# The last projection of the long sequence without Strassen, the order of the jobs around it, and the small steps of four norms on other engines

## The chip, the cores and the metric

The kernel runs on one core of a Trainium2 chip. The metric is the device time of one execution, in microseconds (us); lower is better. The engines are TensorE (PE in the profile; PEld is its weight load), VectorE (DVE), ScalarE (ACT), GpSimd (POOL) and SyncE (SP), which issues the transfers.

## The reference

Two requests pass through the same two layers with shared weights: a prompt of 512 positions (called Q in the kernel) and a sample of 1024 positions (S). The width is 1024. Cut to what matters:

```python
def even_layer(x, ...):                       # layer one
    p = rms_norm(x, g_norm) @ w_in            # value, GLU gate, Fourier input, two gates
    a = a_val * sigmoid(a_glu)
    a = depthwise_conv_centred(a, conv_w)     # 31 taps
    a = silu(layer_norm(a)) * silu(a_z)
    f = real(fft2 over positions and group channels) @ w_four * silu(f_z)
    return x + concatenate([a, f]) @ w_out    # w1o in the kernel

def odd_layer(x, ...):                        # layer two
    u, bg, cg, z = split(rms_norm(x, g_norm) @ w_in, 4)        # w2
    v = depthwise_conv_centred(cg * u, conv_w)                 # 3 taps
    return x + (bg * v * silu(z)) @ w_out                      # w2o

y = rms_norm(odd_layer(even_layer(x)))        # for the prompt and for the sample
```

All of it is in float32.

## The kernel before

**Tiles and precision.** Activations are kept transposed: channels on the 128 partitions, 512 positions (a chunk) along a tile. Q has one chunk and S two. A width of 1024 is 8 such tiles. Each operand of a matmul is split in two parts of a faster format, a high one (a cast on ScalarE, L116 for activations, L144 for weights) and a low one (a subtraction, on VectorE at L110 for activations and on GpSimd at L145 for weights). A product is the sum of high·high, high·low and low·high. So one output tile (`project`, L174 to L190, names `one`, `o`, `val`, `glu`) takes 3 × 8 = 24 matmuls of 128x512. With `kind=1` these are ordered by the input tile k, so that the operands of the last k are needed last.

**Strassen.** For S some projections are done as `Pair` (L656 to L740): two output tiles for both chunks with the Winograd form of Strassen's algorithm, 7 products of 12 matmuls, 84 instead of 96. It needs sums of operands and of weights (VectorE, names `as`, `bs`, `ys`) and sums of results (X, Y, Z at L710, then `xr`). The operands of product p lie in buffer rings by the table `HOME`.

**Order.** The program is written as a list of jobs (`One` for a plain tile, `Pair` for Strassen). `run` (L745) walks through it, loads and splits weights some steps ahead, and advances late generators (vector work of other stages) at given step numbers. A scheduler then places the instructions, and each engine runs its own in order. The jobs are, in the order of the list:

- layer one of Q and S (inputs, 31-tap convolution `conv31`, Fourier part), with Q's output projection
- four groups (j = 0 to 3) of Q's layer-two input, `l2_in`, of four tiles each
- `l1_out_two`: S's output projection of layer one, four pairs
- the other four groups of `l2_in`
- `l2_two`: S's layer-two input, 16 pairs, with the 3-tap convolution and gates
- `l2_out_first`: three tiles of Q's last projection
- `l2_out_two`: S's last projection, four pairs
- `l2_out_last`: Q's other five tiles, each in two halves of 256 columns, so that the first half's final norm runs beside the second half's matmuls. S's final norm (`fin`, 16 output tiles) runs beside them too.

**Norms.** A norm's squares are summed over tiles on ScalarE and VectorE (`SqSum`). `rstd_begin` (L201) sums them over channels by matmuls with a column of ones (`cs`, L209), takes the reciprocal root by a bit trick and three Newton steps on VectorE (12 instructions on at most 8 columns, L214 to L221, ahead of others by priority), and scales a 128x128 identity by it (`d`, L226, one instruction per 128 positions). `rstd_end` (L237) spreads the root over all partitions by a matmul (`r`), and `norm_apply` (L261) scales the tiles. `norm_mid` (L598) is Q's norm between the layers; `layer_norm` (L547) is the one after the 31-tap convolution.

## Time and profile before

| | us |
|---|---|
| median of three runs | 1206.56 |
| lowest and highest | 1206.23, 1209.15 |
| the profiled execution | 1205.27 |
| its span in the trace | 1203.5 |
| PE busy | 1139.1 (95%) |
| DVE busy | 910.3 (76%) |
| POOL busy | 538.7 (45%) |
| ACT busy | 475.3 (39%) |

A row of the timeline gives the start, the duration, the engine, the line, the operation, output<-inputs with their shape, how many such instructions follow each other, and in square brackets the idle time before it with what ended it. In the table of windows each stretch of the span (us) has its length, then for each engine its busy time with the number of instructions, the granted TensorE clock (1 is full), the busy share of the DMA engines and the GB/s that they moved. A row of waits names who waited for whom: us in total, how often, and the longest. In a row that groups instructions stand their count, busy time, mean ns of one, and the idle time before them with what ended it.

The stages in the trace, by window: 150 to 175 us is S's second input norm; 440 to 541 the first four groups of Q's layer-two input; 541 to 627 `l1_out_two`; 627 to 715 the other four groups; 715 to 1034 `l2_two`; 1034 to 1061 the three tiles `l2_out_first`; 1061 to 1145 `l2_out_two`; 1145 to 1184 `l2_out_last`; then the tail.

### The profile page before, as it was taken

Reading aid. Unit: us, or ns where it says so; the run is one execution under the profiler, and the core shown is the slowest. Engines: PE = TensorE matmul, PEld = TensorE weight load, DVE = VectorE, ACT = ScalarE, POOL = GpSimd, SP = SyncE. Lnnn points to the kernel's source line nnn. Section 1 sums busy time; section 2 is a strip of 40 time slices with the busy share of each in tenths; the row PEclk is TensorE's granted clock in tenths of the full one; section 3 lists DMA queues with packets and bytes.
Section 4 is the critical chain, followed back from the end, with each engine's and each line's share of the span. In section 5 each row is a group of like instructions: output and inputs, shape, how many; then the busy total and the mean of one; then the engine's idle time right before and its main releaser. Section 6 shows DMA issues by size and latency. Waiting matters only on the chain. (4 is left out here: it accounts for less than half of the span.)

```text
span 1203.5 us, 15117 instructions
## 1 busy us (share of the span) xinstructions
PE 1139.1 (95%) x5160; PEld 932.6 (77%) x5160; DVE 910.3 (76%) x1306; ACT 475.3 (39%) x827; POOL 538.7 (45%) x396
## 2 busy tenths in 40 slices
PE   7999989999999989997999998999999999979994
PEld 6778868888988868875878876888888888758793
DVE  5899988999899977697564887655546556896756
ACT  6543532223344244443342444333333333643531
POOL 3442532122265535465434544544444544344452
PEclk9999989999999999998999998999999999999997
DMA  9323211111236575355463563221222444766648
GB/s 324 124 95 116 88 53 47 42 53 53 89 106 202 166 243 182 99 185 173 155 219 128 170 211 127 79 88 53 79 71 79 139 133 165 232 208 215 198 155 288
DMA packets 94541, 169.33 MB, mean 141 GB/s; under 512 B 10496, under 2 KB 14080, under 8 KB 94464
## 3 DMA queue, kind: packets, MB, share of 16 engines
q1 hardware_dynamic: 94176, 168.08, 42.9%
q8 instruction: 40, 0.66, 0.2%
q14 instruction: 37, 0.30, 0.1%
q10 hardware_dynamic: 288, 0.30, 0.1%
HBM read 132.94 MB, written 35.39 MB: 140 GB/s over the span
## 5 line engine op out<-in xcount | busy, mean ns | idle before, releaser
L145 POOL TENSOR_TENSOR wo<-wf,wo 128x512 fp32r<-128x512 f32 x254 | 358.1, 1425 | 470.6 <-ACT wo L144 324.7
L144 ACT CAST wo<-wf 128x512 fp32r<-128x512 f32 x256 | 150.1, 618 | 220.5 <-PE X L710 56.2
L145 POOL TENSOR_TENSOR wo<-as,wo 128x512 fp32r<-128x512 f32 x96 | 134.0, 1396 | 136.3 <-ACT wo L144 130.0
L537 DVE SCALAR_TENSOR_TENSOR cv<-a,par_sb,cv 128x1024 f32<-128x1024 f32 x120 | 154.3, 1286 | 2.4 <-ACT cv L535 0.5
L144 ACT CAST wo<-as 128x512 fp32r<-128x512 f32 x96 | 59.3, 618 | 149.0 <-PE X L710 86.9
L710 PE MATMUL X<-ysh,wo 128*128 128x512 f32 x256 | 87.1, 405 | 14.3 <-DVE xr L110 8.0
L537 DVE SCALAR_TENSOR_TENSOR cv<-ap,par_sb,cv 128x512 f32<-128x512 f32 x120 | 90.3, 753 | 2.1
L710 PE MATMUL X<-bsh,wo 128*128 128x512 f32 x256 | 85.0, 393 | 0.0
L110 DVE TENSOR_TENSOR acc<-acc,sq 128x512 f32<-128x512 f32 (+1 forms) x77 | 72.2, 946 | 14.5 <-ACT sq L256 13.4
L188 PE MATMUL one<-ysh,wo 128*128 128x512 f32 x304 | 74.8, 396 | 2.9 <-ACT wo L144 2.9
L710 PEld LDWEIGHTS X<-ysh,wo 128*128 128x128 f32 x256 | 49.6, 194 | 28.4 <-ACT wo L144 11.2
L188 PEld LDWEIGHTS one<-ysh,wo 128*128 128x128 f32 x304 | 57.7, 191 | 15.8 <-ACT wo L144 3.7
L188 PE MATMUL one<-nh,wo 128*128 128x512 f32 x256 | 64.5, 396 | 4.3 <-ACT nh L116 3.8
L188 PEld LDWEIGHTS one<-nh,wo 128*128 128x128 f32 x256 | 47.9, 190 | 16.5 <-ACT nh L116 5.8
L710 PEld LDWEIGHTS X<-bsh,wo 128*128 128x128 f32 x256 | 48.5, 189 | 10.7
L710 PE MATMUL X<-ysl,wo 128*128 128x512 f32 x128 | 51.8, 405 | 0.7 <-DVE ysl L110 0.7
L710 PE MATMUL X<-bsl,wo 128*128 128x512 f32 x128 | 50.5, 394 | 0.0
L710 PE MATMUL Z<-bfh,wo 128*128 128x512 f32 x128 | 43.0, 396 | 4.6 <-ACT wo L144 4.6
L710 PE MATMUL Z<-ysh,wo 128*128 128x512 f32 x128 | 42.7, 396 | 3.6 <-ACT wo L144 3.4
L110 DVE TENSOR_TENSOR as<-wf,wf 128x512 f32<-128x512 f32 x38 | 38.2, 1006 | 10.1 <-POOL wo L145 4.0
L710 PE MATMUL Z<-bsh,wo 128*128 128x512 f32 x128 | 44.3, 389 | 0.0
L110 DVE TENSOR_TENSOR xr<-X,xr 128x512 f32<-128x512 f32 x32 | 21.9, 687 | 29.4 <-PE X L710 24.0
(310 smaller groups left out, 2617.9 us busy)
## 6 DMA issues: line engine op xcount, KB each, us to landing
wf<-w SPq DMA_DIRECT2D x224, 256.0 KB, 2.9
wf<-w1o SPq DMA_DIRECT2D x32, 256.0 KB, 3.1
wf<-w2o SPq DMA_DIRECT2D x32, 256.0 KB, 3.6
x1d<-xr SPq DMA_DIRECT2D x24, 256.0 KB, 2.3
x1r<-x1d SPq DMA_DIRECT2D x24, 256.0 KB, 4.0
bf<-bd SPq DMA_DIRECT2D x22, 256.0 KB, 3.6
xr<-x1d SPq DMA_DIRECT2D x19, 256.0 KB, 3.2
x<-xs SPq DMA_DIRECT2D x16, 256.0 KB, 5.3
```

Of the source, the lines that this page charges most:

```text
L110: ins = eng.tensor_tensor(out=out, in0=a, in1=b, op=op)
L144: nc.scalar.copy(hi, t)
L145: eng.tensor_tensor(out=lo, in0=t, in1=hi.bitcast(F32), op=ALU.subtract)
L188: nc.tensor.matmul(out[:, 0:width], a[k], act[k][b][:, cols], start=(n == 0), stop=(n == 3 * KD - 1))
L537: nc.vector.scalar_tensor_tensor(out=acc, in0=src[:, t:t + n], scalar=col(w0 + t), in1=acc, op0=ALU.mult, op1=ALU.add)
L710: nc.tensor.matmul(out, self.w[p][a][:, k * P:(k + 1) * P], self.ops[p][k][b], start=(first and n == 0), stop=(n == 11), skip_group_check= ...
```

## The change

S's last projection is done plainly: `l2_out` makes 8 tiles for chunk 0 and 3 for chunk 1 as `One` jobs, the first tile of each projection that starts at tile 0 ordered by k; chunk 1's other five tiles are the last ones in halves, with the final norm of S's chunk 0 (8 output tiles, all on VectorE) beside them. Q's last projection stands, as eight plain tiles, before `l2_two`, and Q's final norm within it. Of Q's layer-two input six groups (`n1`) stand ahead of `l1_out_two`, and two behind. S's layer norm starts at step 8 of the list, not 3, with the sums over its channels first. A new function `rstd_aside` is used for S's two input norms, Q's layer norm and Q's `norm_mid`: two small steps on VectorE, thirteen on GpSimd, four scalings of the identity on ScalarE. Half of the loads for S's layer-two operands come from another ring, some raw weights too, and `HOME` gives products 6 and 7 the ring H, 4 and 3 the ring F. Matmuls of 512 columns are 4557 instead of 4509, those of 256 columns 386 as before.

```diff
+    def rstd_aside(acc, n):
+        cs = ps_st("cs", 4)
+        for b in range(4):
+            nc.tensor.matmul(cs[:, b:b + 1], acc[:, b * P:(b + 1) * P], ones_r[:, 0:1].bitcast(F32), start=True, stop=True)
+        with tc.high_priority():
+            small = pool.tile([P, 16], F32, name=nm("y"), tag="sg", bufs=3)
+            v, y, t, sh = [small[:, 4 * i:4 * i + 4] for i in range(4)]
+            nc.vector.tensor_scalar(out=v, in0=cs, scalar1=1.0 / n, scalar2=EPS, op0=ALU.mult, op1=ALU.add)
+            nc.vector.tensor_scalar(out=sh.bitcast(I32), in0=v.bitcast(I32), scalar1=1, scalar2=None,
+                                    op0=ALU.logical_shift_right)
+            g = nc.gpsimd
+            g.tensor_scalar(out=y.bitcast(I32), in0=sh.bitcast(I32), scalar1=-1.0, scalar2=float(MAGIC),
+                            op0=ALU.mult, op1=ALU.add)
+            for _ in range(3):
+                tt(t, y, y, ALU.mult, g)
+                tt(t, t, v, ALU.mult, g)
+                g.tensor_scalar(out=t, in0=t, scalar1=-0.5, scalar2=1.5, op0=ALU.mult, op1=ALU.add)
+                tt(y, y, t, ALU.mult, g)
+            d = pg("dg", "d")
+            for b in range(4):
+                nc.scalar.activation(d[:, b * P:(b + 1) * P], ident, AF.Copy, scale=y[:, b:b + 1])
+        return [d]
...
-        return xt, rstd_begin([acc.acc], D)
+        return xt, rstd_aside(acc.acc, D)
...
     def layer_norm(seq):
...
-            th, tl = split(t, "dg", "lt")
-            if seq is S:
-                yield 1
+            halves.append(split(t, ("dg", "T")[c], "lt"))
+        yield 1
+        accs = []
+        for v, (th, tl) in zip(vs, halves):
...
-        ds = rstd_begin(accs, 512)
+        ds = rstd_aside(accs[0], 512) if seq is Q else rstd_begin(accs, 512)
...
     def norm_mid(seq, c, kept):
-        r = rstd_bcast(seq.sm2[c].acc, D)
+        with tc.high_priority():
+            r = rstd_end(rstd_aside(seq.sm2[c].acc, D))[0]
...
-    HOME = {1: "H", 5: "H", 2: "FQ", 6: "F", 7: "F", 4: "H", 3: "H"}
+    HOME = {1: "H", 5: "H", 2: "FQ", 6: "H", 7: "H", 4: "F", 3: "F"}
...
+                    if h == 0:
+                        x = pool.tile([P, CH], F32, name=nm("x1r"), tag="ap", bufs=4)
+                    else:
+                        x = wide[:, c * CH:(c + 1) * CH]
...
+    def norm_out(seq, c, acc, spilled, ring):
+        ds = rstd_begin([acc.acc], D)
         yield 1
+        r = rstd_end(ds)[0]
+        for m in range(KD):
...
+            nc.vector.scalar_tensor_tensor(out=o, in0=o, scalar=col(PC_N3 + m), in1=r, op0=ALU.mult, op1=ALU.mult)
+            nc.sync.dma_start(seq.out[m, c], o)
...
-    def l2_out_first(seq, act, acc, spilled, ms):
+    def l2_out(seq, c, act, acc, ms, spilled=None, halves=None):
         def tile_of(m):
             def run(x):
-                t = ld("xr2", seq.x1[0][m])
+                t = ld("xr2", seq.x1[c][m], "ld" if halves is None else "FQ")
                 tt(t, x, t, ALU.add)
                 acc.add(t)
...
-            return One(w2o, m, act, run)
+            return One(w2o, m, act, run, kind=int(m == 0))
...
-    conv31(S)
     kept = []
     hm = norm_mid(Q, 0, kept)
+    conv31(S)
...
-    n1, nd = 4, 3
+    n1, nd = 6, 3
     parts = [
-        [t for j in range(n1) for t in l2_in(Q, hm, j, parked)],
+        [t for j in range(n1) for t in l2_in(Q, hm, j, parked, j == 0)],
         l1_out_two(S, yo),
-        [t for j in range(n1, KD) for t in l2_in(Q, hm2, j, parked)],
+        [t for j in range(n1, KD) for t in l2_in(Q, hm2, j, parked, j == n1)],
+        l2_out(Q, 0, act_q, acc_q, range(KD), out_q),
         [x for j in range(KD) for x in l2_two(S, ops, j)],
-        l2_out_first(Q, act_d, acc_q, spilled, range(nd)),
+        l2_out(S, 0, act_s[0], acc_s[0], range(KD), out_s),
+        l2_out(S, 1, act_s[1], acc_s[1], range(nd), halves=xt_e),
     ]
-    jobs_out, fin_s = l2_out_two(S, zo)
-    parts.append(jobs_out)
...
-        (0, 1, out_ops_a(S, yo)), (3, 1, two_norms()),
+        (4, 1, out_ops_a(S, yo)), (8, (0, 2, 4, 5, 6, 7, 8, 9, 10, 11, 12), two_norms()),
...
-    l2_out_last(Q, act_e, acc_q, w_e, xt_e, fin_s())
+    l2_out_last(S, 1, act_s[1], acc_s[1], w_e, xt_e, norm_out(S, 0, acc_s[0], out_s, "dp"))
```

The order of VectorE's instructions at Q's middle norm, before. `cv` is the 31-tap convolution of S, `cs`, `y` and `d` are the norm's root (L216 to L226), `ls` is the sum for S's layer norm, `x1r` the tiles that the norm scales:

```order
L221 SCALAR_TENSOR_TENSOR y_688_3812<-cs_687_3807,y_688_3812 128x4
L537 SCALAR_TENSOR_TENSOR cv_686_3774<-a_339_1751,par_sb_66,cv_686_3774 128x1024
L226 TENSOR_SCALAR d_689_3825<-cst_sb_67,y_688_3812 128x128 x4
L537 SCALAR_TENSOR_TENSOR cv_686_3774<-a_339_1751,par_sb_66,cv_686_3774 128x1024
L110 TENSOR_TENSOR ls_784_4098<-ls_784_4098,a_339_1751 128x512
L261 SCALAR_TENSOR_TENSOR x1r_691_3832<-x1r_691_3832,par_sb_66,r_690_3830 128x512
```

The same place now (the scaling of `norm_apply` is at L285):

```order
L561 SCALAR_TENSOR_TENSOR cv_730_3883<-a_339_1757,par_sb_66,cv_730_3883 128x1024 x4
L209 TENSOR_SCALAR y_684_3689<-cs_683_3684 128x4
L561 SCALAR_TENSOR_TENSOR cv_730_3883<-a_339_1757,par_sb_66,cv_730_3883 128x1024
L210 TENSOR_SCALAR y_684_3689<-y_684_3689 128x4
L561 SCALAR_TENSOR_TENSOR cv_730_3883<-a_339_1757,par_sb_66,cv_730_3883 128x1024 x12
L285 SCALAR_TENSOR_TENSOR x1r_687_3712<-x1r_687_3712,par_sb_66,r_686_3710 128x512
```

Of the twelve small steps that stood among the taps two are left on VectorE, the diagonals are gone from it, and the layer-norm sum no longer stands ahead of the scaling. The other steps are now on GpSimd, among the splits of weights (`wo`, L145) and products of the Fourier part (`fh`):

```order
L213 TENSOR_SCALAR y_684_3689<-y_684_3689 128x4
L110 TENSOR_TENSOR y_684_3689<-y_684_3689 128x4 x2
L218 TENSOR_SCALAR y_684_3689<-y_684_3689 128x4
L110 TENSOR_TENSOR y_684_3689<-y_684_3689 128x4
L145 TENSOR_TENSOR wo_656_3529<-wf_657_3530,wo_655_3528 128x512
L110 TENSOR_TENSOR y_684_3689<-y_684_3689 128x4
L145 TENSOR_TENSOR wo_656_3529<-wf_658_3532,wo_655_3528 128x512
L110 TENSOR_TENSOR fh_504_2781<-fh_504_2781,fz_644_3483 128x512
```

So a chain's steps stand in one queue with full tiles.

VectorE at the start of `l1_out_two`, before: `as` are sums of weights for a pair, `ysl` low parts of operands, `y2` the end of a group of Q, `xr` the first result's add:

```order
L110 TENSOR_TENSOR as_928_4772<-wf_908_4678,as_926_4770 128x512
L110 TENSOR_TENSOR y2_935_4813<-one_934_4788,v_919_4728 128x512
L110 TENSOR_TENSOR ysl_941_4824<-a_294_1364,ysh_940_4823 128x512
L110 TENSOR_TENSOR ysl_943_4828<-a_309_1493,ysh_942_4827 128x512
L110 TENSOR_TENSOR as_971_4951<-wf_953_4875,wf_954_4877 128x512
L110 TENSOR_TENSOR xr_930_4780<-X_944_4831,xr_930_4780 128x512
```

And now:

```order
L110 TENSOR_TENSOR as_982_5098<-wf_970_5023,as_980_5096 128x512
L110 TENSOR_TENSOR as_1025_5277<-wf_1007_5201,wf_1008_5203 128x512
L110 TENSOR_TENSOR as_1026_5278<-as_1025_5277,wf_1006_5199 128x512
L110 TENSOR_TENSOR as_1027_5279<-wf_1006_5199,wf_1007_5201 128x512
L110 TENSOR_TENSOR as_1028_5280<-wf_1009_5205,as_1026_5278 128x512
L110 TENSOR_TENSOR y2_989_5139<-one_988_5114,v_973_5054 128x512
L110 TENSOR_TENSOR ysl_995_5150<-a_294_1370,ysh_994_5149 128x512
```

The four sums of the second pair's weights now stand ahead of the last group's end and of the first pair's operands. The last instructions of VectorE ahead of the last sum over channels (`cs`), before, with `acc` the sum of squares, L1091 S's norm outputs and L1131 Q's:

```order
L110 TENSOR_TENSOR x_2043_10229<-o_2042_10204,xr_2041_10202 128x256
L1131 SCALAR_TENSOR_TENSOR x_1950_9663<-x_1950_9663,par_sb,r_10136 128x256
L1131 SCALAR_TENSOR_TENSOR x_2005_9936<-x_2005_9936,par_sb,r_10136 128x256
L1091 SCALAR_TENSOR_TENSOR x_2040_10195<-x_2040_10195,par_sb,cv_9941 128x512
L110 TENSOR_TENSOR acc_8901<-acc_8901,sq_10189 128x256
L1091 SCALAR_TENSOR_TENSOR x_2045_10234<-x_2045_10234,par_sb,cv_9941 128x512
L110 TENSOR_TENSOR acc_8901<-acc_8901,sq_10231 128x256
L214 TENSOR_SCALAR cs_10242<-cs_10242 128x2
```

And now, with L1064 the norm outputs of the last chunk's first half:

```order
L1064 SCALAR_TENSOR_TENSOR x_1932_9856<-x_1932_9856,par_sb,r_10029 128x256
L110 TENSOR_TENSOR x_1960_10080<-o_1959_10055,xr_1958_10053 128x256
L110 TENSOR_TENSOR acc_9583<-acc_9583,sq_10082 128x256
L110 TENSOR_TENSOR x_1964_10112<-o_1963_10087,xr_1962_10085 128x256
L110 TENSOR_TENSOR acc_9583<-acc_9583,sq_10114 128x256
L238 TENSOR_SCALAR cs_10117<-cs_10117 128x2
```

The norm outputs stand ahead of the last two tiles' adds, and none between the last add and the sum.

More of the change, by code (lines that the diff above doesn't have):

```diff
@@ L547, in layer_norm @@
     def layer_norm(seq):
-        accs = []
         vs = [[seq.a[j][:, c * CH:(c + 1) * CH] for j in range(4)] for c in range(seq.nc)]
-        for v in vs:
+        halves = []
+        for c, v in enumerate(vs):
             t = pg("lx", "ls")
@@ L619, in go, with l2_in @@
         def go(self, p):
-            self.then(project("one", self.w, self.act))
-    def l2_in(seq, h, j, parked, homes=("wo", "wo")):
+            self.then(project("one", self.w, self.act, self.kind))
+    def l2_in(seq, h, j, parked, first_tile=False, homes=("wo", "wo")):
         T = seq.T
@@ new lines, in norm_out @@
+        r = rstd_end(ds)[0]
+        for m in range(KD):
+            if ring == "dp":
+                if m % 2 == 0:
+                    wide = dp("x2", 2 * CH)
+                    for h in range(2):
+                        nc.sync.dma_start(wide[:, h * CH:(h + 1) * CH], spilled[m + h])
+                o = wide[:, m % 2 * CH:(m % 2 + 1) * CH]
+            else:
+                o = ld("x2", spilled[m], ring)
+            nc.vector.scalar_tensor_tensor(out=o, in0=o, scalar=col(PC_N3 + m), in1=r, op0=ALU.mult, op1=ALU.mult)
+            nc.sync.dma_start(seq.out[m, c], o)
+            yield 1
@@ L1097, in get_acts, with y2_acts @@
+    def y2_acts(seq, c, acts, tag):
+        for n in range(0, KD, 2):
+            for k in (n, n + 1):
+                t = seq.y2[c][k]
+                acts.append(split(t if k == KD - 1 else ld("y2", t), tag, "ys"))
+            yield 1
     def get_acts(parked, acts, tag):
@@ L1133, in finish, with tail_room @@
             nc.sync.dma_start(seq.out[m, c][:, cols], o)
[L1135 to L1139 removed]
+    def tail_room(ms, w):
         for m in ms:
@@ L1143, in tail_room, with l2_out_last @@
                 yield 1
-    def l2_out_last(seq, act, acc, w, xt, beside):
+    def l2_out_last(seq, c, act, acc, w, xt, beside):
         half = [slice(0, HF), slice(HF, CH)]
@@ L1177, in l2_out_last @@
         with tc.high_priority():
-            finish(seq, 0, rstd_begin([accs[1].acc], D, HF), xt[1], half[1], (0, 1))
+            finish(seq, c, rstd_begin([accs[1].acc], D, HF), xt[1], half[1], (0, 1))
     def park(t, s):
```

182 lines of the change are left out of this document (37 added, 145 removed).

## The prediction

> **What bounds the kernel now.** I read the page first, then the busy time by stages, then what TensorE (PE) waited for, and last the timeline around each of its waits.
>
> ```profile
> span 1203.5 us, 15117 instructions
> PE 1139.1 (95%) x5160; PEld 932.6 (77%) x5160; DVE 910.3 (76%) x1306; ACT 475.3 (39%) x827; POOL 538.7 (45%) x396
> ```
>
> TensorE is busy for 95% of the span, so a change can win only by fewer matmuls or in the remaining 5%. The stages show where those lie:
>
> ```profile
> core 0: us, PE busy (x) PEld busy (x) DVE busy (x) ACT busy (x) POOL busy (x), PEclk, DMA share, GB/s
> 150.00:175.00 25.00, 21.26 (x74) 14.44 (x73) 21.82 (x41) 9.01 (x15) 9.23 (x5) 0.86 0.10 30
> 440.00:541.00 101.00, 95.56 (x409) 75.87 (x407) 80.28 (x116) 47.31 (x81) 50.76 (x32) 0.97 0.54 172
> 541.00:627.00 86.00, 76.19 (x313) 59.60 (x313) 58.25 (x75) 33.76 (x61) 40.49 (x28) 0.96 0.57 183
> 627.00:715.00 88.00, 85.67 (x381) 70.12 (x382) 60.67 (x96) 32.55 (x58) 41.87 (x29) 1.00 0.52 172
> 715.00:750.00 35.00, 29.72 (x111) 23.11 (x112) 27.55 (x34) 14.88 (x28) 19.23 (x12) 0.85 0.42 139
> 750.00:1034.00 284.00, 283.88 (x1247) 233.57 (x1245) 160.93 (x192) 105.75 (x178) 136.34 (x103) 1.00 0.31 103
> 1034.00:1061.00 27.00, 24.78 (x108) 20.20 (x108) 24.01 (x28) 14.98 (x27) 12.61 (x8) 1.00 0.78 247
> 1061.00:1145.00 84.00, 74.74 (x312) 59.19 (x313) 63.78 (x76) 39.75 (x71) 40.80 (x29) 0.98 0.64 204
> 1184.00:1204.00 20.00, 2.87 (x8) 1.72 (x8) 11.16 (x35) 2.92 (x6) 6.71 (x8) 0.55 0.73 261
> ```
>
> From 750 to 1034 us TensorE never rests: 284 us for 1247 matmuls is 0.2277 us each. In the timeline, a stretch without a wait:
>
> ```profile
> 720.22 3.79 PE L188 MATMUL one<-ysh,wo 128*128 128x512 f32 x16
> ```
>
> Less the pipeline's end, about 0.16 us, this is 0.2267 us a matmul, which I use. A stage's loss is its length less its matmuls times 0.2267, which counts both the waits and the matmuls at a lower clock: 8.2 us in 150:175, 8.3 in 440:541 (layer two's input projection of Q, first part), 15.0 in 541:627 (layer one's output of S by Strassen), 1.6 and 9.8 in the next two (second part, and the start of S's layer two), 2.5 and 13.3 in 1034:1145 (three tiles of Q's last projection, then S's by Strassen), and about 20 in the tail.
>
> What TensorE waits for in these stages:
>
> ```profile
> PE Z L710 <- ACT wo L144: 8.1, 5, 3.0
> PE X L710 <- DVE xr L110: 8.0, 2, 4.0
> PE r L237 <- DVE d L226: 7.9, 3, 3.3
> PE cs L209 <- DVE acc L110: 5.7, 1, 5.7
> PE one L188 <- ACT nh L116: 3.8, 2, 2.9
> ```
>
> (us in total, times, longest.) Most rows end at VectorE (DVE), or at a weight split that stands behind it. In long stretches it has slack; the waits stand where a stage's operands are made just in time.
>
> **The change part by part.** I make the sum against the profiled span and carry it to the median: the profiled execution took 1205.27 us for its span of 1203.5, and the median is 1206.56, so span plus 3.1.
>
> *S's last projection, plain.* Four Strassen pairs of 84 matmuls become 16 tiles of 24: 384 for 336, 48 more, which the instruction orders confirm (4509 to 4557 of 512 columns, the 256-column ones unchanged). 48 × 0.2267 = **+10.9 us**. The orders show 64 vector operations on whole tiles fewer, those that Strassen needed, and the two losses of 1034:1145 go: 2.5 + 13.3 = **−15.8 us**; Q's three tiles stay as work but run beside other jobs.
>
> *New seams.* Two plain projections now start on operands made just before: Q's tile 7 after the last group of Q, S's after the last pair. Both first tiles are ordered by k, so that 21 matmuls (4.8 us) cover the last operand's add, cast and subtraction. Seams of this kind now:
>
> ```profile
> 714.87 3.64 PE L188 MATMUL one<-ysh,wo 128*128 128x512 f32 x8 [2.33 <-ACT wo L144]
> 1035.55 0.50 PE L710 MATMUL Z<-bfh,wo 128*128 128x512 f32 x1 [1.67 <-ACT wo L144]
> ```
>
> The lower price is 1.67 us each. The upper is 2.33 plus a slow start (3.64 − 8 × 0.2267 = 1.8), 4.2 us. I take the middle, 3 each: **+6 us** (3.3 to 8.4). The Trainium skill, "TensorE: Matmul & The Clock Gate", Part 1, has the clock halved only after an idle window of some 3.4 us. By that page both seams would cost only their waits, an estimate of +4; the row at 714.87 disagrees, its eight matmuls ran near half speed after 2.33 us.
>
> *The tail.* The last big matmuls now belong to S's second chunk, in the same five tiles of two halves; beside them stand 8 norm outputs on VectorE instead of 16 that also used GpSimd (POOL). Before:
>
> ```profile
> 1182.29 1.12 PE L188 MATMUL o<-ysh,wp 128*128 128x256 f32 x8
> 1191.37 0.98 PE L209 MATMUL cs<-ones_r,acc 128*128 128x1 f32 x4 [5.69 <-DVE acc L110]
> 1186.78 0.42 DVE L110 TENSOR_TENSOR x<-o,xr 128x256 f32<-128x256 f32 x1
> 1187.12 1.65 DVE L1131 SCALAR_TENSOR_TENSOR x<-x,par_sb,r 128x256 f32<-128x256 f32 x4
> 1190.33 0.89 DVE L110 TENSOR_TENSOR acc<-acc,sq 128x256 f32<-128x256 f32 x1
> ```
>
> From the last matmul's end (1183.41) to the sum over channels (1191.37) pass 8.0 us, since the last tile's add and squares stand behind norm outputs in VectorE's queue. In the new order nothing stands between the last add and its sum: add 0.42, square 0.42, sum 0.42 and three hand-overs, about 3 us. What follows keeps its length. **−5 us** (−6 at best; 0 if VectorE is still late).
>
> *Small steps of the chains.* The reciprocal roots of S's two input norms, Q's layer norm and Q's middle norm keep two steps on VectorE, send 13 to GpSimd and the four diagonals to ScalarE. The trace has no such GpSimd step; its nearest rows:
>
> ```profile
> 145.33 0.17 DVE L214 TENSOR_SCALAR cs<-cs 128x4 f32<-128x4 f32 x1
> 155.37 0.87 DVE L226 TENSOR_SCALAR d<-cst_sb,y 128x128 f32<-128x128 f32 x4
> 156.38 2.05 PE L237 MATMUL r<-d,ones_r 128*128 128x512 f32 x2 [3.34 <-DVE d L226]
> L145 POOL TENSOR_TENSOR wo<-wf,wo 128x512 fp32r<-128x512 f32 x254 | 358.1, 1425 | 470.6 <-ACT wo L144 324.7 <-issue 21.6 <-DVE xr L110 20.5
> L1129 POOL TENSOR_TENSOR x<-x,rs 128x256 f32<-128x256 f32 x6 | 4.2, 724 | 6.1 <-ACT rs L1124 6.1
> L385 POOL MEMSET es<- 128x2 f32 x4 | 0.4, 100 | 0.0
> ```
>
> 512 columns cost 1.425 us, 256 cost 0.724: by that line four columns cost about 0.03 us, and the smallest POOL row is 0.1. The upper bound is a full tile's 1.425. A chain's four columns are nearest to the MEMSET; I take 0.2 us with the hand-over, 13 × 0.2 = 2.6 us. But POOL's queue is in order, and weight splits stand between the steps: five full tiles within the middle norm's chain, 5 × 1.4 = 7 us. With that a chain lasts about 10 us, against 10.0 on VectorE now (145.33 to 155.37). The Trainium skill, "GPSIMD Engine Reference", section 3.1, gives a dispatch cost of about 156 ns for each instruction as VectorE's side of its table, with more hops on GpSimd; by an estimate of 0.2 to 0.3 us a step from that page the sum keeps its sign, and its advice (section 4.1: elementwise work on VectorE) speaks against this part. For the second input norm of S the gain is then that VectorE's other work no longer stands in the chain: of 3.34 us and the slow matmuls after it I take **−1.5 us** (+15.5 for steps of 1.425: 18.5 + 7 − 10; −3 if the wait goes).
>
> *Start of Q's layer-two input.* Three rows of VectorE set it:
>
> ```profile
> 424.72 1.47 DVE L226 TENSOR_SCALAR d<-cst_sb,y 128x128 f32<-128x128 f32 x4
> 429.85 1.65 DVE L110 TENSOR_TENSOR ls<-ls,a 128x512 f32<-128x512 f32 x1 [2.46 <-ACT a L545]
> 432.58 2.72 DVE L261 SCALAR_TENSOR_TENSOR x1r<-x1r,par_sb,r 128x512 f32<-128x512 f32 x4 [1.08 <-PE r L237]
> 447.59 2.06 PE L188 MATMUL one<-nh,wo 128*128 128x512 f32 x3 [2.92 <-ACT nh L116]
> ```
>
> The chain was interleaved with the 31-tap convolution, a step behind each tap, and the scaling waited behind S's layer-norm sum, whose operand ScalarE was still copying. Now that sum starts four groups later in the job list and is gone from this place, so the scaling moves forward by about 5 us (429.85 − 2.46 to 432.58). The stage loses 8.3; I take **−4 us** (0 to −6.5).
>
> *Six groups ahead of layer one's output.* Two more groups are 8 × 24 × 0.2267 = 43.5 us of cover in which VectorE can do S's layer norm, gates and Strassen operands. Before:
>
> ```profile
> 541.96 0.50 PE L710 MATMUL X<-ysh,wo 128*128 128x512 f32 x1 [1.56 <-ACT wo L144]
> 556.41 0.77 PE L710 MATMUL X<-ysh,wo 128*128 128x512 f32 x1 [3.99 <-DVE xr L110]
> ```
>
> The second wait holds a result back while VectorE is in weight sums and operand subtractions. The new order has the second pair's four weight sums ahead of the first pair's late operands, so they are done in the cover. Of 15.0 us lost I take a third, **−5 us** (0 to −10): the rest is adds and splits within the stage, which stay.
>
> *Bridge to S's layer two.* Its loads now come through two buffer rings, and beside it stand two groups and Q's eight tiles of the last projection, whose vector work is lighter. Before:
>
> ```profile
> 711.76 0.62 ACT L116 CAST bh<-x1r 128x512 fp32r<-128x512 f32 x1 [5.42 <-DVE x1r L865]
> 739.37 0.62 ACT L116 CAST bfh<-bf 128x512 fp32r<-128x512 f32 x1 [6.45 <-DMA bf<-bd]
> 743.00 4.01 DVE L110 TENSOR_TENSOR bfl<-bf,bfh 128x512 fp32r<-128x512 f32 x4
> ```
>
> The 743.00 row is behind a parked operand's reload, which still goes through one ring. I take half of 9.8, **−5 us** (0 to −9.8). The moved loads I cost at nothing beside these jobs: 1034:1061 already shows 247 GB/s.
>
> Sum: 10.9 − 15.8 + 6 − 5 − 1.5 − 4 − 5 − 5 = **−19.4 us**; 1206.56 − 19.4 = **1187 us**.
>
> **Rivals.** *The waits come back elsewhere* (chance 0.17). VectorE is 68 to 89% busy in the stages with the losses (58.25 of 86, 24.01 of 27), and a wait taken at one place returns at the next. Then only the projection, its seams and the tail count: 10.9 − 15.8 + 6 − 5 = −3.9, **1203 us**. Against it speaks that two of the gains come from removed or moved-off work, not only from order.
>
> *GpSimd becomes the late engine* (0.13). Four chains of 13 dependent steps at up to 1.425 us are 18.5 us each, with 7 us of weight splits between: 25 for 10. Three of these chains have little PE work beside them; if half of their 3 × 15.5 us shows, +23 takes the place of −1.5 and −4: −19.4 + 5.5 + 23 = +9.1, **1216 us**, slower. It decides from 0.94 us a step (half of 3 × (13 × 0.94 + 7 − 10) is the 13.9 that is left); the 724 ns row for 256 columns speaks against that.
>
> *Every seam closes* (0.12): all ends at their best, 10.9 − 15.8 + 3.3 − 6 − 3 − 6.5 − 10 − 9.8 = −36.9, **1170 us**. The stretch from 750 to 1034 shows that such a pace is possible; but seams with a parked reload are still there.
>
> That the change doesn't do what it says can be left out: the orders show the 48 matmuls and the moved steps.
>
> **How the numbers follow.** The main case has 0.58, with a range of its own of 1175 to 1198. With 1203 and 1216 at 0.30 together and 1170 at 0.12, a range from 1172 to 1206 leaves out the slower rival and about half of the best case: 2 in 10. Within 0.3% (3.6 us, about what this measurement can tell) ends at 1202.9; the 1203 case lies on that edge, 0.07 below and 0.10 above. Faster: 0.58 + 0.12 + 0.07 = 0.77; same: 0.10; slower: 0.13.
>
> **What would show it.** Plain last projection right: 48 more matmuls, the wait for xr near the end gone, and each seam 1.7 to 4.2 us. Tail: last big matmul to the sum over channels about 3 us. Chains: GpSimd steps on four columns at 0.1 to 0.3 us, and no longer wait for the diagonals than 3.3 us. Starts: the loss before layer one's output of S below 10 us, and that of Q's layer-two input near 4. Wrong, if POOL's small steps take 0.7 us or more, if weight casts become PE's chief wait during Q's tiles, or if the plain S projection shows a wait in each tile for its residual load.

## The result, and the profile after

The changed kernel takes 1176.38 us (median of four runs, 1174.50 to 1180.38) where the kernel before takes 1207.86 (four runs, 1206.23 to 1209.33). The ratio is 0.9744, with a 95% interval of 0.9712 to 0.9776: 31 us less, 2.6%. The forecast was 1187 us in a range of 1172 to 1206. The profiled execution has a span of 1173.2 us, 30.3 less than before, with 48 matmuls more. A second profile of the same kernel, taken in another sitting, has a span of 1175.9. Of all runs told here one was slow, one of four with seven groups (a granted clock of 0.846, 1272.91 us), and it stands in no ratio.

The busy time by stages after the change (columns as before: length, then PE, PEld, DVE, ACT and POOL busy, clock, DMA share, GB/s). The stages are S's second input norm, Q's first six groups, layer one's output of S, the last two groups with Q's last projection, the start of S's layer two, most of the rest of it, its end with most of S's last projection (whose first tile starts at 1072), the last five tiles in halves with what comes just before them, and the tail:

```profile
150.00:175.00 25.00, 21.96 (x82) 15.86 (x82) 22.51 (x33) 9.26 (x16) 11.48 (x6) 0.93 0.21 64
435.00:574.00 139.00, 136.21 (x603) 111.67 (x602) 98.79 (x140) 63.72 (x109) 74.36 (x51) 1.00 0.52 169
574.00:652.00 78.00, 73.15 (x314) 58.12 (x312) 53.00 (x67) 33.54 (x59) 36.73 (x27) 1.00 0.56 183
652.00:752.00 100.00, 97.10 (x428) 78.90 (x429) 80.98 (x119) 42.22 (x75) 50.40 (x34) 1.00 0.65 213
752.00:788.00 36.00, 31.16 (x129) 24.27 (x128) 24.52 (x46) 14.31 (x25) 14.25 (x11) 0.95 0.58 187
788.00:1064.00 276.00, 276.00 (x1213) 227.56 (x1212) 149.77 (x178) 103.77 (x174) 134.72 (x102) 1.00 0.25 83
1064.00:1123.00 59.00, 58.70 (x264) 48.43 (x263) 24.41 (x29) 23.48 (x41) 26.98 (x21) 1.00 0.67 214
1123.00:1160.00 37.00, 36.36 (x273) 34.41 (x272) 27.50 (x64) 12.14 (x25) 16.29 (x14) 1.00 0.45 150
1160.00:1174.00 14.00, 1.80 (x6) 1.02 (x6) 5.47 (x22) 0.79 (x2) 1.41 (x2) 0.61 0.33 112
```

Counted as in the prediction (length less matmuls times 0.2267), the first six stages lose 6.4, 2.3, 6.8, 3.0, 6.8 and 1.0 us, and 1064:1123 nothing: 264 × 0.2267 is 59.8, a little over its 59, since eight of the 264 have one column only. That row is the clearest of the table: TensorE is busy for 58.70 of 59 us, where 1061:1145 before had 74.74 of 84.

Some of PE's waits after (the longest of all, 6.5 us at the very start, was 6.4 before):

```profile
PE one L188 <- ACT wo L144: 4.4, 4, 1.5
PE r L261 <- DVE d L250: 3.0, 1, 3.0
PE glu L188 <- ACT nh L116: 2.9, 1, 2.9
PE X L738 <- DVE xr L110: 2.7, 2, 1.9
PE cs L233 <- DVE acc L110: 1.9, 2, 1.7
```

The wait for `xr` fell from 8.0 to 2.7 us in total, that for the diagonal `d` from 7.9 in three waits to 3.0 in one, that for the last sum of squares from 5.7 to 1.9. The waits of 2.9 us for `nh` and of up to 1.5 us for weights (two of them within Q's six groups, at 550 and 557 us) stand at new places.

The page's first row tells more than the waits do: PE was busy for 1139.1 us before and is for 1133.5 after, though 48 matmuls were added (10.9 us). So some 16.5 us were saved by matmuls that no longer run at the lower clock behind a wait; the mean granted clock rose from 0.977 to 0.993. In the second profile PE is busy for 1138.0 us at a clock of 0.990, so there it is 12.0 us. A wait that goes is worth more than its length.

### The profile page after: what moved, and what is told of

Same layout as the page of the kernel before. It is cut to its first block, busy times and chain, and to the rows that moved or that the text cites. A ratio compares the mean times of both kernels' runs of the same rounds, so it can differ in the third digit from the quotient of the medians.

```text
span 1173.2 us, 15069 instructions
## 1 busy us (share of the span) xinstructions
PE 1133.5 (97%) x5208; PEld 934.7 (80%) x5208; DVE 858.3 (73%) x1202; ACT 469.2 (40%) x821; POOL 538.7 (46%) x448
## 5 line engine op out<-in xcount | busy, mean ns | idle before, releaser
L145 POOL TENSOR_TENSOR wo<-wf,wo 128x512 fp32r<-128x512 f32 x274 | 377.1, 1393 | 445.3 <-ACT wo L144 310.9
L145 POOL TENSOR_TENSOR wo<-as,wo 128x512 fp32r<-128x512 f32 x80 | 111.8, 1397 | 121.5 <-ACT wo L144 120.4
L188 PE MATMUL one<-ysh,wo 128*128 128x512 f32 x432 | 110.6, 393 | 1.9 <-ACT wo L144 1.6
L188 PE MATMUL one<-nh,wo 128*128 128x512 f32 x384 | 93.9, 391 | 2.8 <-ACT wo L144 2.8
L188 PEld LDWEIGHTS one<-ysh,wo 128*128 128x128 f32 x432 | 80.5, 188 | 20.2 <-ACT wo L144 2.4
L188 PEld LDWEIGHTS one<-nh,wo 128*128 128x128 f32 x384 | 71.9, 188 | 18.7 <-ACT wo L144 3.6
L188 PE MATMUL one<-ysl,wo 128*128 128x512 f32 x216 | 58.3, 390 | 0.5 <-DVE ysl L110 0.5
L188 PE MATMUL one<-nl,wo 128*128 128x512 f32 x192 | 49.3, 392 | 0.0
L188 PEld LDWEIGHTS one<-ysl,wo 128*128 128x128 f32 x216 | 40.6, 188 | 9.4 <-DVE ysl L110 0.9
L110 DVE TENSOR_TENSOR mc<-X,mc 128x512 f32<-128x512 f32 x24 | 16.6, 692 | 38.3 <-PE X L738 38.3
L738 PE MATMUL X<-ysh,wo 128*128 128x512 f32 x128 | 41.9, 392 | 2.7 <-DVE xr L110 2.7
```

Of the source, the lines that this page charges most:

```text
L110: ins = eng.tensor_tensor(out=out, in0=a, in1=b, op=op)
L145: eng.tensor_tensor(out=lo, in0=t, in1=hi.bitcast(F32), op=ALU.subtract)
L188: nc.tensor.matmul(out[:, 0:width], a[k], act[k][b][:, cols], start=(n == 0), stop=(n == 3 * KD - 1))
L738: nc.tensor.matmul(out, self.w[p][a][:, k * P:(k + 1) * P], self.ops[p][k][b], start=(first and n == 0), stop=(n == 11), skip_group_check= ...
```

## The experiments

Each ratio is to the kernel before in the same sitting. Its medians there were 1209 to 1210 us, so 0.974 of it is some 1178.

**The changed kernel again.** No edit; it is the measure for the runs beside it.

> The changed kernel once more, beside the kernel before, as the measure for the runs of the same sitting: 0.974 of the kernel before.

1177.04 us, ratio 0.9738 (0.9711 to 0.9764), as expected.

**The chains back on VectorE.**

```diff
     def rstd_aside(acc, n):
-        cs = ps_st("cs", 4)
-        ...
+        return rstd_begin([acc], n)
```

> The changed kernel with the four chains of small steps back on VectorE. By the milestones of the two traces, the start of the input projection of S's second chunk moved forward by 4.7 us, of which 1.1 stand at the kernel's very start; the stage of Q's first layer-two groups gained 7.0 us. Theory A, the moved steps free VectorE and the path: 3.5 us come back at the two input norms and some 2 to 4 of the 7.0 at the middle norm, 1182 to 1184 us. Rival B, the order of the jobs made the gain and the place of 52 small steps is worth nothing: 1176 to 1178.

1179.72 us, ratio 0.9748 (0.9721 to 0.9776). The ratio lies between A and B and isn't told apart from that of the changed kernel. The wait for the diagonal at S's second norm is back, in the timeline of this kernel:

```profile
157.18 2.01 PE L240 MATMUL r<-d,ones_r 128*128 128x512 f32 x2 [3.34 <-DVE d L229]
```

In the changed kernel there is no wait at that matmul; a few matmuls later it waits for the next thing in the chain, the scaled tile's high part:

```profile
155.24 0.50 PE L188 MATMUL glu<-nh,wo 128*128 128x512 f32 x1 [2.94 <-ACT nh L116]
```

So most of the wait moved on by one step. VectorE's own order is why. In the changed kernel the root is spread by 151.4 us (the `r` matmuls start at 150.32 and take 1.12), but the scaling stands behind 11 taps of the convolution and two more instructions:

```profile
143.96 8.67 DVE L561 SCALAR_TENSOR_TENSOR cv<-ap,par_sb,cv 128x512 f32<-128x512 f32 x11
153.80 5.35 DVE L285 SCALAR_TENSOR_TENSOR x<-x,par_sb,r 128x512 f32<-128x512 f32 x8
```

That `glu` matmul starts at 159.25 us in the second profile of the changed kernel and at 160.68 with the chains on VectorE: 1.4 us. At Q's middle norm this kernel lost nothing much: 139 us for 599 matmuls in 440:579, 3.2 us, against 2.3. There the chain's place is worth little once S's layer-norm sum is out of the way.

**The chains alone, in the kernel before.**

```diff
+    def rstd_aside(acc, n): ...
-        return xt, rstd_begin([acc.acc], D)
+        return xt, rstd_aside(acc.acc, D)
-        ds = rstd_begin(accs, 512)
+        ds = rstd_aside(accs[0], 512) if seq is Q else rstd_begin(accs, 512)
-        r = rstd_bcast(seq.sm2[c].acc, D)
+        with tc.high_priority():
+            r = rstd_end(rstd_aside(seq.sm2[c].acc, D))[0]
```

> The kernel before with the four chains alone moved to GpSimd and ScalarE. Theory A: 3.5 us at the input norms, and at the middle norm little, since S's layer-norm sum still stands ahead of the scaling: 1203 to 1205 us. Rival B, the steps are worth nothing by themselves: 1207 to 1209. Rival C, GpSimd's queue is in the way without the later changes: above 1209.

1206.77 us, ratio 0.9967 (0.9950 to 0.9984): 3 to 4 us less than its neighbours, clear of no change. Theory A has the direction and about the size (1206.77 lies between its range and B's), and rival C falls. The trace has 744 matmuls done in the first 175 us, against 724 before, but this count can't show the gain: two profiles of one program, the changed kernel, have 745 and 727 there, for a reason that the last section shows. The stage 150:175 is steadier. It has 82 matmuls in this trace and in both profiles of the changed kernel, and 74 to 77 in the six traces with the chains on VectorE: 5 to 8 matmuls, 1.1 to 1.8 us.

At the middle norm little is left in the end, as theory A had it, but not for its reason. The chain's new place moves Q's start a good deal, and then TensorE waits at S's layer norm; the same matmul here and in the kernel before:

```profile
474.04 0.80 PE L583 MATMUL mu<-lth,lnmean 128*128 128x512 f32 x1 [3.71 <-ACT lth L116]
480.91 0.50 PE L559 MATMUL mu<-lth,lnmean 128*128 128x512 f32 x1 [0.49 <-ACT lth L116]
```

The matmul ahead of `mu` starts at 469.83 for 480.04, 10.2 us earlier, and `mu` itself 6.9 earlier; 1.3 us are left at the end of the span (1202.2 for 1203.5).

**Four groups ahead in place of six.**

```diff
-    n1, nd = 6, 3
+    n1, nd = 4, 3
-        (4, 1, out_ops_a(S, yo)), (8, (0, 2, 4, 5, 6, 7, 8, 9, 10, 11, 12), two_norms()),
+        (0, 1, out_ops_a(S, yo)), (3, 1, two_norms()),
...
-        (at[2] + 1, (0, 1, 2, 4, 5, 8, 9, 10, 11), l2_ops(S, ops, far)),
-        (at[2] + 2, (0, 1, 2, 3, 6), y2_acts_q(parked, act_q)),
+        (at[4] - 15, (0, 1, 2, 4, 5, 8, 9, 10, 11), l2_ops(S, ops, far)),
+        (at[3] - 6, (0, 1, 2, 3, 6), y2_acts_q(parked, act_q)),
```

> The changed kernel with four groups of Q ahead of layer one's output of S and four behind, and S's layer norm started at step 3 as before; all else as changed. Theory A, the cover of the two groups made the gains at the start of Q's layer two (7.0 us, the layer norm's sum out of the way) and in S's output of layer one (6.8): most of the 13.8 us comes back, 1186 to 1190 us. Rival B, lighter VectorE chains and the later rings made them: 1177 to 1180.

1186.26 us, ratio 0.9814 (0.9775 to 0.9852), 0.7% or some 8.5 us slower than the changed kernel (the edit also starts S's layer norm at step 3 again and moves two late generators). That is theory A for layer one's output of S, but not for the start of Q's layer two: 435:535 loses 100 − 422 × 0.2267 = 4.3 us, so of the gain there (8.3 to 2.3) two thirds stay without the two groups. Its timeline shows two waits that the six groups cover, at S's layer norm (0.49 before, as shown above) and at the first result's add (3.99 before):

```profile
463.31 0.65 PE L585 MATMUL mu<-ltl,lnmean 128*128 128x512 f32 x1 [3.70 <-DVE ltl L110]
552.05 0.77 PE L738 MATMUL X<-ysh,wo 128*128 128x512 f32 x1 [6.49 <-DVE xr L110]
```

and by its windows layer one's output of S loses 86 − 306 × 0.2267 = 16.6 us, against 6.8:

```profile
535.00:621.00 86.00, 75.09 (x306) 60.33 (x306) 59.06 (x74) 34.77 (x62) 39.72 (x27) 0.92 0.53 172
```

The second row of the timeline is instructive. This kernel too has the second pair's weight sums ahead of the first result's add, as the changed one. With that order and without the cover the wait is longer (6.49 us for 3.99 before). With both it is 1.86, in the changed kernel:

```profile
583.98 0.47 PE L738 MATMUL X<-ysh,wo 128*128 128x512 f32 x1 [1.86 <-DVE xr L110]
```

So the order by itself was not the gain; the 43.5 us of matmuls ahead of it (8 tiles of 24) were.

**Seven groups.**

```diff
-    n1, nd = 6, 3
+    n1, nd = 7, 3
-        (at[2] + 2, (0, 1, 2, 3, 6), y2_acts_q(parked, act_q)),
+        (at[2], (0, 1, 2, 3, 4), y2_acts_q(parked, act_q)),
```

> The changed kernel with seven groups of Q ahead of layer one's output of S and one behind it. Theory A, the cover ahead of that stage is still short and the bridge to S's layer two needs its own: the stage loses 2 to 4 us less, the bridge with 12 jobs in place of 16 up to 10 more: 1178 to 1186 us. Rival B, sixteen jobs in the bridge were more than needed: 1173 to 1177, faster than the changed kernel.

1180.51 us (the middle one of three runs), ratio 0.9742 (0.9696 to 0.9788), not told apart from six groups. By its windows the stage and the bridge move the way that theory A has it, by less than it said:

```profile
600.00:677.00 77.00, 73.91 (x318) 58.77 (x317) 53.73 (x68) 33.01 (x59) 37.44 (x27) 1.00 0.57 185
677.00:757.00 80.00, 75.75 (x336) 61.10 (x334) 67.28 (x101) 33.07 (x58) 37.74 (x25) 1.00 0.70 229
757.00:793.00 36.00, 29.83 (x115) 23.49 (x116) 31.04 (x54) 16.02 (x29) 14.74 (x10) 0.86 0.59 188
```

Layer one's output loses 4.9 us, the bridge 3.8 + 9.9 = 13.7, where the changed kernel's bridge lost 3.0 + 6.8 = 9.8. What one place gains, the other pays: six is about the middle.

**S's last projection plain, at its old place.** The kernel before, with 16 plain tiles of S between Q's three and five.

```diff
-    jobs_out, fin_s = l2_out_two(S, zo)
+    _, fin_s = l2_out_two(S, zo)
...
+    jobs_out, acc_s, xt_s = l2_out_plain(S, act_s)
...
-        (at[4] - 6, 1, l2_out_early(S, zo, zfar, act_d, parked)),
-        (at[4] - 1, 1, l2_out_mid(S, zo, zfar)),
-        (at[5], 1, l2_out_late(S, zo, zfar)),
+        (at[4] - 6, 1, get_acts(parked, act_d, "H")),
+        (at[4], 1, y2_plain(S, 0, act_s[0])),
+        (at[5] + 1, 1, y2_plain(S, 1, act_s[1])),
```

> The kernel before with S's last projection plain at the same place (between Q's three and five tiles), all else as before. 48 more matmuls cost 10.9 us; the Strassen stage lost 13.3 us against its matmuls; the new seam lies behind Q's three tiles, so about 1 us. Theory A: 10.9 - 13.3 + 1 = -1.4, 1205 to 1208 us: the plain form by itself is nearly even, and the gain at the end came from the order (S last) and the seam in front. Rival B, VectorE freed from the sums gives more, also within the layer before it: 1195 to 1201.

1213.95 us, ratio 1.0039 (1.0017 to 1.0060): slower by 4 to 5 us. Neither theory had that. The plain stage itself loses as little as theory A said, but behind it a new wait stands:

```profile
1053.00:1149.00 96.00, 93.90 (x413) 76.50 (x412) 38.03 (x49) 40.10 (x72) 42.71 (x32) 1.00 0.80 256
1149.00:1194.00 45.00, 40.10 (x287) 37.32 (x287) 23.97 (x66) 15.05 (x29) 19.93 (x15) 0.96 0.54 171
```

```profile
1154.41 2.07 PE L188 MATMUL one<-ysh,wo 128*128 128x512 f32 x4 [4.88 <-ACT wo L144]
1148.59 1.21 ACT L144 CAST wo<-wf 128x512 fp32r<-128x512 f32 x2 [5.83 <-DMA wf<-w2o]
```

413 matmuls in 96 us leave 2.4 us of loss in front of 1149 us, for 15.8. Then the weights of Q's last five tiles come late (ScalarE, which casts them, waits for their transfers), and these tiles take 45 us, for 39 before.

**The same, those weights asked for earlier.**

```diff
-        (at[6] - 3, 1, tail_room(range(nd, KD), w_e, spilled, xt_e))])
+        (at[6] - 7, 2, tail_room(range(nd, KD), w_e, spilled, xt_e))])
```

> The kernel with S's last projection plain at its old place, with the weights of Q's five last tiles asked for four jobs earlier. Theory A, the plain form at that place lost by the wait of 4.9 us for these weights and the slow matmuls behind it: that wait goes, 1207 to 1210 us, even with the kernel before. Rival B, the weights are late because the plain tiles use up the ring of raw weights and the queue: the wait stays, 1213 to 1215.

1217.57 us, ratio 1.0071 (1.0050 to 1.0092): no gain, if anything slower than the run before it, so theory A falls; the time is beyond rival B's as well. The wait only moved to the front, into the plain tiles, where ScalarE's queue has the weights' casts behind those of Q's reloaded operands (`ac`), which wait for their transfers too:

```profile
1129.02 3.78 PE L188 MATMUL one<-ysh,wo 128*128 128x512 f32 x8 [5.89 <-ACT wo L144]
1112.99 0.62 ACT L116 CAST ysh<-ac 128x512 fp32r<-128x512 f32 x1 [6.14 <-DMA ac<-yd]
```

In this stretch operands of S, operands of Q, residuals and weights come through one queue, which moves 162.57 MB of the run before this one and all other queues 1.3 (at 256 GB/s, 80% of the DMA engines, in 1053:1149). So the plain form was no gain by itself: its 10.9 us were spent, and about half of the losses it removed came back, 6 us, in the tiles behind it. In the changed kernel, with Q's projection elsewhere, no reload of Q's operands stands there, the stage moves 214 GB/s, and there is no such wait. Whether the queue, ScalarE's order or one ring of buffers sets this wait wasn't tried by itself.

**More work on GpSimd, side by side.** Three idle instructions on four columns behind each Newton step.

```diff
+            def slow():
+                for _ in range(3):
+                    tt(idle[:, 0:4], v, v, ALU.mult, g)
             for _ in range(3):
                 tt(t, y, y, ALU.mult, g)
+                slow()
```

> The changed kernel with three idle steps on four columns added behind each of the twelve Newton steps on GpSimd, so that each step costs four times its 0.2 us: 36 steps of 0.2 us, 7.2 us more in each of the four chains. Theory A, the chains of S's two input norms lie on the path and the other two are covered: 7 to 14 us more than the changed kernel. Rival B, the queue of GpSimd has room everywhere: within 2 us of it. Rival C, all four lie on the path: 20 to 29 us more.

1176.19 us, ratio 0.9729 (0.9703 to 0.9756), as the changed kernel: rival B by the number, but the edit didn't do what was meant. The timeline of GpSimd shows why:

```profile
149.68 0.20 POOL L110 TENSOR_TENSOR id<-y 128x4 f32<-128x4 f32 x1
149.83 0.20 POOL L110 TENSOR_TENSOR y<-y 128x4 f32<-128x4 f32 x1
153.32 6.28 POOL L110 TENSOR_TENSOR id<-y 128x4 f32<-128x4 f32 x23
```

No step of the chain waits for an idle instruction (`id`). One went between each two steps, where the next step follows only after 0.27 us anyway, and here, at S's second norm, 23 of the others stand behind the chain. It grew by 0.4 us (from its first step on GpSimd to its last 3.75, for 3.36), not 7.2. This run says nothing on whether the chains are on the path.

**Longer chains.** Twelve Newton steps for three.

```diff
-            for _ in range(3):
+            for _ in range(12):
                 tt(t, y, y, ALU.mult, g)
```

> The changed kernel with twelve Newton steps in place of three in each chain on GpSimd: 36 more dependent instructions. In the trace of the changed kernel a dependent one follows the last after 0.27 us (145.39 to 148.94 for 13), so each chain grows by 9.7 us. Theory A, the chains of S's two input norms lie on the path: 10 to 19 us more than the changed kernel, 1187 to 1196. Rival B, GpSimd's chains are covered wherever they stand: within 3 us of 1177. Rival C, all four on the path: 1205 or more.

1199.92 us, ratio 0.9918 (0.9887 to 0.9948): some 22 us more than the changed kernel by the ratios, between A and C. Rival B falls. Its timeline:

```profile
167.04 2.08 PE L261 MATMUL r<-d,ones_r 128*128 128x512 f32 x2 [7.85 <-ACT d L222]
453.15 2.11 PE L188 MATMUL one<-nh,wo 128*128 128x512 f32 x4 [1.49 <-ACT nh L116]
461.69 0.73 PE L188 MATMUL one<-nh,wo 128*128 128x512 f32 x2 [2.78 <-ACT nh L116]
```

In the first 175 us 681 matmuls are done, against 727 in the second profile of the changed kernel: 10.4 us for the two input norms. Q's first groups lose 8 us more (453:594 has 577 matmuls in 141 us, 10.2, against 2.1 in that second profile), so the middle norm is on the path as well as soon as it grows. Q's layer norm is not: this run is 11.4 us behind the second profile ahead of that norm (170.60 us for 159.25 at the same matmul) and 10.9 just behind it (274.94 for 264.02).

The edit did more than was expected of it. From a chain's first GpSimd step to its last it takes 5.7, 3.4, 6.5 and 9.4 us in the changed kernel and 24.0, 17.1, 19.5 and 27.5 here, 13 to 18 us more and not 9.7: the longer a chain, the more full tiles stand between its steps (two, none, two and five in the changed kernel; eight, three, four and twelve here). Of these 63 us some 22 came through.

**The first tiles not ordered by k.**

```diff
-        return [One(w2, m, h, f, homes[n % 2], int(n == 0 and first_tile))
+        return [One(w2, m, h, f, homes[n % 2], 0)
-            return One(w2o, m, act, run, kind=int(m == 0))
+            return One(w2o, m, act, run, kind=0)
```

> The changed kernel with the first tiles of its plain projections not ordered by k, so that the last operand is needed after 7 matmuls (1.6 us) and not after 21 (4.8 us). Theory A, the new seams are small because of this order: up to 3.2 us back at each of the four starts (two of Q's layer-two input, Q's and S's last projection), 4 to 12 us more. Rival B, the operands are early anyway: within 2 us of the changed kernel.

1180.24 us, ratio 0.9761 (0.9729 to 0.9792), 3.2 us above the changed kernel in the same sitting, between the two theories; the ranges of the runs don't overlap (1178.91 to 1181.07, 1176.41 to 1177.94). Of four starts one pays, where Q's projection begins:

```profile
710.95 3.31 PE L188 MATMUL one<-ysh,wo 128*128 128x512 f32 x7 [1.96 <-ACT wo L144]
```

Seven matmuls took 3.31 us, half speed behind a wait of 1.96. At the other three the trace has no wait of over 0.8 us.

**The tail of the kernel before: outputs earlier.**

```diff
-            for _ in range(1 if i == 0 else 3):
+            for _ in range(3):
                 next(beside, None)
```

> The kernel before with S's sixteen norm outputs taken three at a time beside the last tiles from the first half on, so that none is left behind the last tile's add. Theory A, they held the last sum back: the 8.0 us from the last matmul to the sum over channels fall to 4 to 6 (four outputs of Q's first half still stand there), 1204 to 1206 us for 1208. Rival B, the same vector work only moves ahead and delays other tiles: no gain.

1213.87 us, ratio 1.0025 (1.0004 to 1.0047): rival B, if anything slower. No norm output of S stands behind the last add any more, and yet the last sum comes later, 9.8 us after the last matmul's end (1185.79 to 1195.58):

```profile
1184.67 1.12 PE L188 MATMUL o<-ysh,wp 128*128 128x256 f32 x8
1190.91 1.19 PE L237 MATMUL r<-d,ones_r 128*128 128x256 f32 x2 [5.12 <-DVE d L226]
1195.58 0.98 PE L209 MATMUL cs<-ones_r,acc 128*128 128x1 f32 x4 [3.47 <-DVE acc L110]
```

The outputs now stand between the small steps of the first half's root, for whose diagonal TensorE waits 5.1 us (1.60 before), and the last adds stand behind that.

**The tail with half of the outputs.** The final scaling of S's second chunk is left out; its tiles are copied as they are.

```diff
             for c, r in enumerate(rs):
+                if c == 1:
+                    for m in range(KD):
+                        nc.sync.dma_start(seq.out[m, c], xt[c][m])
+                    break
```

> The kernel before with the final scaling of S's second chunk left out: its eight tiles go to the output unscaled, so VectorE and GpSimd have eight norm outputs beside the last tiles and not sixteen. Theory A, the tail was long because sixteen outputs don't fit beside ten half tiles: from the last matmul to the sum over channels 3 us and not 8, 1203 to 1205 us for 1209. Rival B, the order on VectorE made it long, whatever their number: within 1.5 us of before.

1210.76 us, ratio 1.0010 (0.9989 to 1.0031). In the trace the tail is what theory A said: from the last matmul's end (1189.48) to the sum 4.3 us, for 8.0:

```profile
1188.36 1.12 PE L188 MATMUL o<-ysh,wp 128*128 128x256 f32 x8
1193.78 0.99 PE L209 MATMUL cs<-ones_r,acc 128*128 128x1 f32 x4 [3.86 <-DVE acc L110]
```

The time is not: the 3.7 us gained there are lost in front of it, since the last matmul ends 6.1 us later than before. By the starts of the same matmuls 4.1 us are lost by the end of layer one's output of S (541:628, 309 matmuls, 16.9 us of loss for 15.0), in stages whose order is the same as before; so two executions differ by as much as the term in question. This kernel is 1.0 us late at 1121.58 (the time in the trace before), and 5.7 at 1144.83, behind a wait that the kernel before doesn't have there:

```profile
1146.68 0.50 PE L710 MATMUL Z<-ysh,wo 128*128 128x512 f32 x1 [2.94 <-ACT wo L144]
```

The added copies are issued from 1095 us on, so they may be part of that second loss. That wasn't tried by itself.

## Why the prediction was right, and where its terms were off

The forecast of 1187 us was for faster, and the case that came is the main one, near the fast end of its own range (1175 to 1198), with its terms on the whole too small: a sum of −19.4 us where −31 were measured. The right direction is not luck of errors that cancel, since nearly all of them lie to one side. Losses by windows of the first profile after, all us:

| term | predicted | measured |
|---|---|---|
| 48 matmuls | +10.9 | +10.9 by their count (with the plain form alone PE is busy for 1151.1, 12.0 more than before, its slow matmuls included) |
| losses of the old last projection | −15.8 | −15.8 (no loss left) |
| new seams | +6 | +2.4 (2.1 at Q's, 0.3 at S's) |
| tail | −5 | −6.5 (20.1 from the last matmul's end, now 13.6) |
| S's second norm, and the first | −1.5 | −0.7 to −4.8 (727 and 745 matmuls in 0:175, 724 before); the second alone −1.1 to −1.8 |
| start of Q's layer two | −4 | −6.0 (−4.0 with four groups) |
| layer one's output of S | −5 | −8.2 |
| bridge to S's layer two | −5 | −3.7 (11.4 before; 9.8 now, less Q's seam) |

These are single traces. Layer one's output of S, from its first matmul to its last, takes 84.5 us in the profile before and 86.7 to 89.3 in the five other traces of kernels edited from it; it takes 77.7 and 79.1 in the two after. So by most executions this stage gained more than the table says.

The *seams* are the term that was most off in proportion. They were priced from seams of the kernel before, but the start of S's projection has one wait of 0.30 us, and Q's has these, in the changed kernel's timeline:

```profile
1073.85 0.73 PE L188 MATMUL one<-ysh,wo 128*128 128x512 f32 x2 [0.30 <-ACT ysh L116]
714.20 0.50 PE L188 MATMUL one<-ysl,wo 128*128 128x512 f32 x1 [0.52 <-DVE ysl L110]
733.97 2.11 PE L188 MATMUL one<-ysh,wo 128*128 128x512 f32 x8 [0.66 <-ACT wo L144]
740.62 2.12 PE L188 MATMUL one<-ysh,wo 128*128 128x512 f32 x8 [0.92 <-ACT wo L144]
```

Q's are 2.1 us in all (they stand in the bridge's windows and are taken out of its row), and the matmuls behind them keep their pace (8 in 2.11 us). The 4.8 us of cover by the order over k, which the prediction named, did the work at Q's start: without that order 3 us come back there.

The two *starts* were taken too small for the same reason. I took half or a third of a stage's loss where the mechanism removed most or half. The mechanism was right for layer one's output of S: the six groups are worth 8.5 us, nearly all there (16.6 us lost without them, 6.8 with them). But I read the new order of the weight sums as part of the gain, and in the run with four groups the wait behind that order is longer than before. Q's start needed two things together. With the chains moved alone it came earlier, and S's layer-norm sum made TensorE wait instead (3.71 us); with that sum moved, the chain's place was worth about 1 us.

The *bridge* was taken a little too large. The parked operand's reload is still just in time (1.6 us there for 2.1), and a wait for a copy on ScalarE (`mc`, 2.3 us) is new.

The *tail* had the right size and an incomplete reason. I had named the norm outputs behind the last add. Taking those away alone makes the tail longer; halving their number shortens it to 4.3 us, and the changed kernel has 1.7:

```profile
1158.45 1.12 PE L188 MATMUL o<-ysh,wp 128*128 128x256 f32 x8
1161.26 0.58 PE L233 MATMUL cs<-ones_r,acc 128*128 128x1 f32 x4 [1.70 <-DVE acc L110]
```

So the number of instructions beside the last ten half tiles counts, not only their place. That the last 2.6 us come from the same cause is argued, not shown.

The *last projection* was costed rightly as a whole, −15.8 + 10.9, but I credited the plain form with what needed the order too: at the old place the same form is 4 to 5 us slower than Strassen.

The *small steps* last what I took, 0.2 us, in the changed kernel's groups:

```profile
L110 POOL TENSOR_TENSOR y<-y 128x4 f32<-128x4 f32 x36 | 7.4, 205 | 2.6
```

But one follows the other only after 0.27 us, and the chain as a whole was wrong. I took the middle norm's (five full tiles between the steps, about 10 us) for all. That one takes 9.4 us from its first GpSimd step to its last; the one of S's second norm, which I priced, has no tile between its steps and takes 3.4. From its first small step on VectorE to its diagonals pass 6.5 us (146.52 to 152.98 in the second profile), for 10.0 before. The gain is no larger than I took because VectorE's taps hold the scaling back after it.

The Trainium skill, "GPSIMD Engine Reference", section 4.1, would have left them on VectorE. The one run that moved nothing else gained 3 to 4 us, so here the measurement decides against that advice: VectorE is busy for 21.82 of the 25 us of 150:175 before, GpSimd for 9.23.

Of the rivals, "the waits come back elsewhere" fell: the waits in all are fewer, and only the bridge (7.7 of 11.4 us) and S's second norm (6.4 of 8.2) kept most of their loss. Its mechanism shows where one part was moved alone: 3.71 us at S's layer norm with the chains, 4.88 us for weights with the plain projection. "GpSimd becomes the late engine" fell at 0.2 us a step, but its mechanism is real: it put +23 on three chains 15.5 us longer, and four chains 13 to 18 us longer cost some 22. "Every seam closes" (1170) was 6 us from the time and the main case's 1187 was 11, though the first had a chance of 0.12.

Not tried by themselves are the other buffer rings, Q's last projection ahead of S's layer two, and the plain projection at its new place with the tail that it makes. The last of these, −9.0 us by the table (the rows of the matmuls, the old losses, the seams and the tail), is read from the traces alone.

## What to carry to other kernels

Price a wait with the slow matmuls behind it, since 16.5 of the 41 us that were saved here (30.3 and the 10.9 spent) were clock in one profile, and 12.0 of 38.5 in the other; and where a stage's operands are made just in time, put independent matmuls ahead of it before you reorder the late engine's queue. A form with fewer vector operations and more matmuls pays only where its loads have room: the same plain projection was a loss beside the other sequence's reloads and part of a gain apart from them. Test a chain on another engine by making the chain itself longer, not by adding instructions that can slip into its gaps, and measure in the trace by how much it grew.

## What the runs showed of the hardware

**The same wait may or may not halve the clock.** Two profiles of the same changed kernel, in the stretch 80:104 us, the first and the second:

```profile
80.00:104.00 24.00, 21.96 (x118) 18.69 (x118) 23.93 (x44) 13.28 (x26) 8.10 (x7) 1.00 0.42 132
87.56 0.71 PE L470 MATMUL z<-wcs,eo 128*128 128x128 f32 x4 [1.76 <-DVE x L285]
90.27 2.00 PE L188 MATMUL az<-rh,wo 128*128 128x512 f32 x8
```

```profile
80.00:104.00 24.00, 21.95 (x98) 18.27 (x97) 20.32 (x36) 11.11 (x21) 7.69 (x6) 0.86 0.36 113
88.38 0.71 PE L470 MATMUL z<-wcs,eo 128*128 128x128 f32 x4 [1.76 <-DVE x L285]
92.11 3.62 PE L188 MATMUL az<-rh,wo 128*128 128x512 f32 x8
```

The wait is 1.76 us in both. Behind it eight matmuls take 2.00 us in one and 3.62 in the other; from 90 to 92 us the granted clock is 1.00 in the first and 0.50 in the second. The waiting matmuls start 0.8 us apart in the two traces (87.56 and 88.38), and those behind the eight 3.4 apart (92.11 and 95.52): some 3 us between executions of one program, from the clock alone. This is why the table gives a range for the first norms. The Trainium skill, "TensorE: Matmul & The Clock Gate", Part 1, says that the window over which activity is measured runs freely, so that the same kernel meets it in other phases; these rows agree with that. They don't agree with its length as the least wait that matters (some 3.4 us): 1.76 us with a few small matmuls behind it was enough in one of the two.

**Small instructions on GpSimd overlap.** On four columns each takes 0.20 us by itself. In a chain they follow each other after 0.27 us (145.39 and 145.66 us in the changed kernel). In the run with the idle instructions, where a step of the chain and an idle one take turns, the rows start 0.15 us apart; the 23 idle ones that stand alone, which all write the same four columns, follow each other after some 0.27 again (6.28 us for 23). So a chain leaves room between its steps for other small work, at 0.4 us for a whole chain.
